# A hybrid attention and delta-net block on one core: w_out by token rows with resident, pre-gated slabs

## The chip, the core and the metric

The kernel runs on one core of a Trainium2 chip. A core has a matrix engine (TensorE, "PE" in the profile, with its weight loads shown as "PEld"), three engines for elementwise work (VectorE "DVE", ScalarE "ACT", GpSimd "POOL"), and SyncE ("SP"), which here issues most of the transfers between HBM and the on-chip memory SBUF. Matrix products land in PSUM, eight banks of 128 partitions by 512 floats. Every engine runs its own list of instructions in order and waits on semaphores for the others.

The metric is the device time of one execution in microseconds (us), the median of the runs shown; lower is better. A profile is one further execution, recorded by the hardware.

## What is computed

One transformer block for 1024 tokens of width D = 1024, in float32. A vector c modulates it: `mod` is silu(c) times a matrix `w_ada` plus `b_ada`, cut into six vectors of width 1024. Left out below are the two mixers, a dilated attention (8 heads of 64) and a gated delta rule (8 heads of 64).

```python
def _rmsnorm(x, g):
    x32 = x.astype(jnp.float32)
    y = x32 * lax.rsqrt(jnp.mean(x32 * x32, axis=-1, keepdims=True) + EPS)
    return (y * g.astype(jnp.float32)).astype(x.dtype)
...
        mod = c_act @ w_ada[l] + b_ada[l]
        sh1, sc1, g1, sh2, sc2, g2 = [m[:, None, :] for m in jnp.split(mod, 6, axis=-1)]
        h = _rmsnorm(x, norm_attn_g[l]) * (1.0 + sc1) + sh1
...
        y = jnp.concatenate([y_attn, y_delta], axis=-1) @ w_out[l]
        x = x + g1 * y
        h = _rmsnorm(x, norm_ffn_g[l]) * (1.0 + sc2) + sh2
        y = (jax.nn.silu(h @ w_gate[l]) * (h @ w_up[l])) @ w_down[l]
        x = x + g2 * y
    return _rmsnorm(x, final_norm_g)
```

The change concerns the product with `w_out`, the gate `g1` behind it and the norm, scale and shift that make h for the feed-forward part.

## The kernel before

**Products.** Each float32 operand is split into a high part that TensorE takes in one pass (fp32r) and the low remainder, and a product is the sum of three: high by high, high by low, low by high. One instruction multiplies a stationary 128x128 tile with a moving 128x512 tile. `wsplit` (L228) brings a slab of weights of 128 x 512: SP's transfer, ACT's cast to the high part, POOL's subtraction for the low part (L237).

**Stages.** Projections and the delta rule run first (to about 470 us). Then comes attention: 32 units, four pairs of heads by eight query blocks. A unit's scores are made by `att_score`, normalised on POOL (tile X, L1273), transposed one unit later by `att_turn` (L1285, blocks "tr"), and multiplied with the values three units later by `att_value` (L1301). Between those products TensorE is given others: a generator in `fill[0]`, from which `ahead` draws as many steps as a share of time allows. Up to unit 8 (`i == free`) these are leftover projections; at that point a change of hands takes place: old pools close, the operands yh and yl (the mixers' outputs, transposed, high and low) are allocated and loaded, and the filler becomes `out_delta`.

**w_out in two phases.** `out_delta` multiplies the delta half of y with its half of w_out, 16 groups of 12 products, each giving one tile [128 output columns, 512 tokens]: the weights are stationary and y moves. DVE multiplies the group with the gate (a column of `mod`) and adds x (L1367); the result goes to HBM (`xp`). After attention, phase 2 (L1481 to L1541) does the same for the attention half, 16 groups in order of token half and column block d, each slab of weights loaded again for each half; DVE multiplies with the gate and adds the loaded `xp` tile (L1492). Each x tile is also turned to rows by four transposes two groups later (`x2_turn`, L1449) and written to HBM as `x2`.

**The norm by columns.** Since a tile holds columns on its partitions, the sum of squares over D runs across partitions: ACT squares, POOL and DVE accumulate (L1504), eight matmul records take the sum for four token blocks (L1514), then a root and a reciprocal, a diagonal tile dg (L1517) and a product with ones that spreads the factors over the partitions (rsb, L1521). `normed2` applies factor and scale on DVE (L1533) and the shift on ACT (L1536), in place.

**After w_out.** H11 and H21 are the split halves of the first 512 tokens' h; the gate and up products of the first two column blocks ("early", L1700, through `gate_first`, `up_first` and `up_mm`, L1574) need only these. The rest of the up and gate products uses sums of blocks in the manner of Strassen: DVE makes T1, T2, T3, T4 and H22 from the x2 tiles by subtractions and splits (L1705 on; lines L1580, L1583 and L1470). The second half's `normed2` calls stand in the loop that makes T2. Then the feed-forward network runs to the end.

**Modulation.** `mod_in` loads one 128x512 tile of w_ada ("wm"), `mod_add` adds its product with c to an accumulator on DVE (L1335), and every eighth addition `mod_out` sums over partitions by four products with ones (L1345). 16 additions stand before the attention loop, then one per iteration from the third on.

**Order.** A scheduler orders instructions by the program's order and by priorities: code under `urgent()` goes ahead, and `tc.issue_after` puts transposes behind a named product. So each engine's list, which is fixed before the kernel runs, decides who waits behind whom.

Of the kernel before, what the change touches and what calls it, by code (L numbers as in the profile page):

```python
# [88 lines left out]
def build(tc, I, out):  # L89
# [68 lines left out]
    def tbank(name):  # L158
        return psb(name, "t", 2)
# [32 lines left out]
    G2 = const([P, KT], "G2")  # L192
    R_d = dr.tile([8, 1152], F32, name="R_d")
# [340 lines left out]
    class _:  # L534
# [13 lines left out]
        xp = scratch("xp", 2 * KT, [P, HALF])  # L548
# [78 lines left out]
    def z_evac(g):  # L627
        def f(tb, ps):
            zt = pv.tile([P, 256], F32, name=f"zt{g}_{tb}", tag="zt", bufs=4)
# [457 lines left out]
    def va_evac(c):  # L1087
        def f(tb, ps):
            t = pv.tile([P, 256], F32, name=f"va{c}_{tb}", tag="vt", bufs=4)
# [5 lines left out]
    def spill(name, dst):  # L1095
        def f(hf, ps):
            for i in range(2):
                t = pv.tile([P, 256], F32, name=f"sp_{name}_{hf}_{i}", tag="vt", bufs=4)
# [99 lines left out]
    for tag, n, w in (  # L1198
        ("X", XB, T), ("raw", 2, T), ("QS", 3, T), ("KS", 3, T), ("va", 2, T), ("KL", 3, T), ("et", ETB, T),
        ("ng", 2, T), ("xo", 3, HALF), ("wm", 4, HALF),  # L1200
# [119 lines left out]
    def mod_in(n):  # L1320
        if n < 64:
            i, k = n // KT, n % KT
            t0 = 16 + 4 * i
            p, b = (pa, 4) if i < 6 else (po2, 2)
            mod_w[n] = p.tile([P, HALF], F32, name=f"wm_{i}_{k}", tag="wm", bufs=b)
# [13 lines left out]
    def mod_out(i):  # L1339
        t0 = 16 + 4 * i  # L1340
        acc = states[:, HALF * (i % 2) : HALF * (i % 2) + HALF]
        ps = tbank(f"mods{i}")
        v = acc.rearrange("p (t j m) -> p j t m", j=4, m=32)
# [4 lines left out]
        t = (pv if i < 6 else po2).tile([P, 256], F32, name=f"mt{i}", tag="zt", bufs=4 if i < 6 else 1)  # L1348
# [6 lines left out]

    def out_delta():

        for d in range(KT):
            slabs = [(wsplit(I["wo"][d, 1], 512, f"wo{d}_1"), 4)]
            for hf in range(2):  # L1360
                cs = slice(hf * HALF, (hf + 1) * HALF)
                xo = pa.tile([P, HALF], F32, name=f"xo{d}_{hf}", tag="xo", bufs=3)
                nc.sync.dma_start(xo, I["xT"][d * P : (d + 1) * P, cs])
                ps = gbank(f"wo{d}_1_{hf}")
                yield from gemm(ps, slabs, yh, yl, cs)
                with urgent():
                    nc.vector.scalar_tensor_tensor(  # L1367
                        out=xo, in0=ps, scalar=mod[:, 16 + d : 17 + d], in1=xo, op0=ALU.mult, op1=ALU.add,
                    )
                nc.sync.dma_start(_.xp[2 * d + hf], xo)  # L1370
# [14 lines left out]
    for n in range(4):  # L1385
        mod_in(n)
    ahead(LEAD)
    for n in range(16):
        mod_add(n)
        mod_in(n + 4)  # L1390
    for i in range(len(units) + AV):
        if i >= AV:
            mod_add(16 + i - AV)
        if i == free:
            run(fill[0])
            share[0] = 0.0
            sh_.close()
            py, sy = pool("py", side="right")
# [24 lines left out]
        if i in (1, 2):  # L1423
            mod_out(i - 1)
        if i >= AV:
            if 20 + i - AV < 48:
                mod_in(20 + i - AV)
            if (i - AV) % 8 == 7:
                mod_out(2 + (i - AV) // 8)
# [6 lines left out]
    run(fill[0])  # L1436

# [7 lines left out]
    def x2_turn(d, hf, t):  # L1445

        ps = tbank(f"x2t{d}_{hf}")
        for b in range(4):
            nc.tensor.transpose(ps[:, b * P : (b + 1) * P], t[:, b * P : (b + 1) * P], ident)  # L1449
        xt = px.tile([P, 4, P], F32, name=f"xt2_{d}_{hf}", tag="m", bufs=5)  # L1450
        nc.scalar.copy(xt.rearrange("p b d -> p (b d)"), ps)
        nc.sync.dma_start(
            _.x2[hf][:, :, d * P : (d + 1) * P].rearrange("b p d -> p b d"), xt
        )

    behind = []
    x2 = {}
# [18 lines left out]
    acc = px.tile([P, HALF], F32, name="acc2_0", tag="m", bufs=5)  # L1476
# [4 lines left out]
    for hf in range(2):  # L1481
        cs = slice(hf * HALF, (hf + 1) * HALF)
        if hf == 1:
            acc = px.tile([P, HALF], F32, name="acc2_1", tag="m", bufs=5)
        for d in range(KT):
            slabs = [(wsplit(I["wo"][d, 0], 512, f"wo{d}_0_{hf}"), 0)]
            t = x2[d, hf]
            nc.sync.dma_start(t, _.xp[2 * d + hf])
            ps = (gbank, sbank)[d % 2](f"wo{d}_0_{hf}")
            run(gemm(ps, slabs, yh, yl, cs))  # L1490
            with urgent():
                nc.vector.scalar_tensor_tensor(  # L1492
                    out=t, in0=ps, scalar=mod[:, 16 + d : 17 + d], in1=t, op0=ALU.mult, op1=ALU.add,
                )
            behind.append((d, hf, t))
            if len(behind) > 2:
                with tc.issue_after(last[0].ins):
                    x2_turn(*behind.pop(0))
            if d == 0:
                nc.scalar.activation(acc, t, AF.Square)  # L1500
            else:
                sq = px.tile([P, HALF], F32, name=f"sq2_{hf}_{d}", tag="m", bufs=5)
                nc.scalar.activation(sq, t, AF.Square)
                (nc.vector if d > 5 else nc.gpsimd).tensor_tensor(out=acc, in0=acc, in1=sq, op=ALU.add)  # L1504
        while behind:
            x2_turn(*behind.pop(0))

        ps, pb = ybank(f"ssq2_{hf}"), abank(f"rsb2_{hf}")
        r4 = r8[:, 4 * hf : 4 * hf + 4]
        rs = po.tile([P, HALF], F32, name=f"rs2_{hf}", tag="p1", bufs=4)  # L1510
        dg = po.tile([P, 4, P], F32, name=f"dg2_{hf}", tag="p1", bufs=4)
        with urgent():
            for tb in range(4):
                nc.tensor.matmul(ps[:, tb : tb + 1], acc[:, tb * P : (tb + 1) * P], ones[:, 0:1], start=True, stop=True)  # L1514
            nc.scalar.activation(r4, ps[:, 0:4], AF.Sqrt, bias=eps1, scale=1.0 / D)
            nc.vector.reciprocal(r4, r4)
            nc.vector.tensor_tensor(  # L1517
                out=dg, in0=ident.unsqueeze(1).to_broadcast([P, 4, P]),
                in1=r4.unsqueeze(2).to_broadcast([P, 4, P]), op=ALU.mult,
            )  # L1520
            nc.tensor.matmul(pb, ones, dg.rearrange("p b t -> p (b t)"), start=True, stop=True)  # L1521
            nc.scalar.copy(rs, pb)
        if hf == 1:
            sy.close()
            spv.close()
            wq, swq = pool("wq", side="right")
            pt, st_ = pool("pt", side="right")
            for name in ("H22", "T1", "T2", "T3", "T4"):
                h2_block(pt, name)

        def normed2(d):
            t = x2[d, hf]
            nc.vector.scalar_tensor_tensor(  # L1533
                out=t, in0=t, scalar=G2[:, d : d + 1], in1=rs, op0=ALU.mult, op1=ALU.mult
            )
# [426 lines left out]
```

## Time and profile before

| | us |
|---|---|
| median of 3 runs (1408.3 to 1410.0) | 1409.6 |
| the profiled execution | 1412.03 |
| its span, first to last instruction | 1410.3 |
| TensorE busy | 1344.1 (95%) |
| VectorE busy | 930.7 (66%) |
| ScalarE busy | 660.5 (47%) |
| GpSimd busy | 291.2 (21%) |
| mean granted TensorE clock | 0.987 of full speed |

How to read the rows that follow: a group row gives line, engine, operation, `output<-inputs`, shapes and count, then busy us and mean ns of one, then the idle time of the engine just before them and what ended it. A timeline row gives start, duration, engine, line and tiles, in brackets the idle time before it and its releaser. A row of waits reads "who waited for whom: us in total, times, longest". The chain of waits follows back from the last instruction to what released each step.

### The profile page before, as it was taken

To read this page: it belongs to the slowest core of one execution; us is meant where nothing else is said; L and a number is where in the kernel's file an instruction comes from. 1 tells how busy PE (TensorE), PEld (TensorE's weight loads), DVE (VectorE), ACT (ScalarE), POOL (GpSimd) and SP (SyncE) were. 2 spreads that over 40 slices of the span, in tenths; PEclk is the share of its full clock that TensorE was granted. 3 is DMA by queue.
4 is the path that set the end of the run, shared out by engine and by line. 5 is a ranking of instruction groups with operands and counts; after the bars stand their busy time and mean duration, and the time that the engine had idled before them with its cause. 6 is when DMAs were issued, how large, how long until landed. Compare 5 with 4: busy or idle time off the path is not lost.

```text
span 1410.3 us, 23618 instructions
## 1 busy us (share of the span) xinstructions
PE 1344.1 (95%) x8536; PEld 1106.0 (78%) x8536; DVE 930.7 (66%) x1739; ACT 660.5 (47%) x1274; POOL 291.2 (21%) x262
## 2 busy tenths in 40 slices
PE   7998999999998899999999799999999999999997
PEld 4776887888898777777877588888888888888886
DVE  3687694658546266866549986767575776474487
ACT  3487434374333446555568433333333333444446
POOL 2335432434314433444351000000000000000000
PEclk9999899999999999999999899999999999999999
DMA  8645334463403887673274375545363665766677
GB/s 305 219 132 163 90 115 132 129 186 87 131 24 100 261 254 243 211 223 120 79 225 131 124 220 172 166 142 185 114 217 110 201 208 180 264 214 201 195 221 244
DMA packets 171342, 244.59 MB, mean 173 GB/s; under 512 B 33014, under 2 KB 76327, under 8 KB 171224
## 3 DMA queue, kind: packets, MB, share of 16 engines
q1 hardware_dynamic: 156504, 231.53, 52.2%
q10 hardware_dynamic: 14720, 11.54, 2.5%
q8 instruction: 67, 1.10, 0.3%
q14 instruction: 51, 0.42, 0.1%
HBM read 180.25 MB, written 67.48 MB: 176 GB/s over the span
## 4 chain that ended last, share of the span: by engine, by line
PE 67%; DVE 15%; DMA 8%; issue 4%; ACT 3%; POOL 2%; SPq 1%; ACTq 0%; DVEq 0%; POOLq 0%
PE wua L1574 8%; PE wga L1574 8%; PE X L1777 7%; PE wuc L1574 4%; PE Z L1777 4%; PE wgc L1574 4%; PE wo L595 4%; PE g_a L595 2%; DMA wm<-in_wada 2%; PE Y L1777 2%; DVE tm L894 2%; DVE tt L898 2%; PE wgb L1574 2%; PE wub L1574 2%; PE f L257 2%
## 5 line engine op out<-in xcount | busy, mean ns | idle before, releaser
L1564 DVE TENSOR_TENSOR wl_db<-wr_db,wh_db 128x512 fp32r<-128x512 f32 x77 | 53.2, 691 | 75.6 <-ACT wh_db L1563 75.4
L1563 ACT CAST wh_db<-wr_db 128x512 fp32r<-128x512 f32 x77 | 47.9, 622 | 98.0 <-PE X L1777 42.9
L1271 ACT ACTIVATE X<-X,sc 128x128 f32<-128x128 f32 (+7 forms) x64 | 49.7, 777 | 71.5 <-DVE sc L1266 60.8
L1273 POOL TENSOR_SCALAR X<-X,sc 128x128 f32<-128x128 f32 (+7 forms) x64 | 51.6, 807 | 112.4 <-DVE sc L1272 83.2
L1777 PE MATMUL X<-wl_db,wh_da 128*128 128x512 f32 x176 | 68.7, 390 | 0.3 <-DVE wl_db L1564 0.2
L1777 PE MATMUL X<-wh_db,wl_da 128*128 128x512 f32 x176 | 68.5, 389 | 0.0
L1777 PE MATMUL X<-wh_db,wh_da 128*128 128x512 f32 x176 | 68.4, 389 | 0.0
L1335 DVE SCALAR_TENSOR_TENSOR states<-wm,cc,states 128x512 f32<-128x512 f32 x56 | 46.5, 831 | 17.0 <-DMA wm<-in_wada 16.2
L595 PE MATMUL wo<-yh,wh_wo 128*128 128x512 f32 x128 | 54.0, 422 | 0.0
L1564 DVE TENSOR_TENSOR wl_da<-wr_da,wh_da 128x512 fp32r<-128x512 f32 x77 | 52.8, 686 | 1.7 <-ACT wh_da L1563 1.7
L1266 DVE CUSTOM_DVE_ANT_0 X<-S,ng 128x512 f32<-128x512 f32 (+3 forms) x64 | 37.4, 585 | 22.2 <-PE S L1263 18.4
L595 PE MATMUL g_a<-hh,wh_a 128*128 128x512 f32 x128 | 51.4, 401 | 0.0
L595 PE MATMUL wo<-yh,wl_wo 128*128 128x512 f32 x128 | 51.2, 400 | 0.0
L595 PE MATMUL wo<-yl,wh_wo 128*128 128x512 f32 x128 | 51.0, 398 | 0.0
L595 PE MATMUL g_a<-hh,wl_a 128*128 128x512 f32 x128 | 50.8, 397 | 0.0
L595 PE MATMUL g_a<-hl,wh_a 128*128 128x512 f32 x128 | 50.7, 396 | 0.0
L1563 ACT CAST wh_da<-wr_da 128x512 fp32r<-128x512 f32 x77 | 47.4, 616 | 6.5 <-PE wua L1574 5.8
L1285 PE MATMUL tr<-ident,X 128*128 128x128 f32 x288 | 43.7, 279 | 6.1 <-DVE et L1288 4.8
L1563 ACT CAST wh_wg_s<-wg_s 128x512 fp32r<-128x512 f32 x33 | 20.5, 623 | 59.9 <-PE wuc L1574 22.6
L1285 PEld LDWEIGHTS tr<-ident,X 128*128 128x128 f32 x288 | 33.0, 141 | 14.8 <-issue 3.6
L1563 ACT CAST wh_wg<-wr_wg 128x512 fp32r<-128x512 f32 x33 | 20.5, 622 | 51.1 <-PE wua L1574 18.9
L1563 ACT CAST wh_wu_s<-wu_s 128x512 fp32r<-128x512 f32 x33 | 20.4, 621 | 49.6 <-PE wga L1574 16.7
(527 smaller groups left out, 4377.0 us busy)
## 6 DMA issues: line engine op xcount, KB each, us to landing
wr_da<-ao_d SPq DMA_DIRECT2D x77, 256.0 KB, 3.2
wm<-in_wada SPq DMA_DIRECT2D x64, 256.0 KB, 3.8
wr_wg<-in_wg SPq DMA_DIRECT2D x48, 256.0 KB, 2.9
wr_wu<-in_wu SPq DMA_DIRECT2D x48, 256.0 KB, 2.7
ao_d<-a SPq DMA_DIRECT2D x44, 256.0 KB, 2.7
wr_wd<-in_wdn SPq DMA_DIRECT2D x44, 256.0 KB, 3.2
wr_db<-wt_d SPq DMA_DIRECT2D x44, 256.0 KB, 3.2
ao_d<-as SPq DMA_DIRECT2D x33, 256.0 KB, 2.0
```

Of the source, the lines that this page charges most:

```text
L257: nc.tensor.matmul(first[bank], a[:, w0], b[k][:, cs], start=(k == 0 and n_ == 0), stop=(k == KT - 1 and n_ == 2))
L595: last[0] = nc.tensor.matmul(ps, a[:, w0], b[k0 + k4][:, cs], start=(i == 0), stop=(i == n - 1))
L894: nc.vector.tensor_tensor(out=tv, in0=bc(nt[:, j, j + 1 : 32], j + 1), in1=tt[:, j, 0 : j + 1].unsqueeze(1).to_broadcast([P, m, j + 1]), o ...
L1266: nc.vector.tensor_tensor_reduce(out=X[:, c0:c1], in0=ps[:, 0 : c1 - c0], in1=ng[:, u + c0 : u + c1], scale=1.0, scalar=(3e38 if m is None ...
L1271: nc.scalar.activation(X[:, 0:nk], X[:, 0:nk], AF.Exp, scale=-1.0, bias=m, accum_out=sc[:, 2:3])
L1273: nc.gpsimd.tensor_scalar(out=X[:, 0:nk], in0=X[:, 0:nk], scalar1=sc[:, 3:4], scalar2=0.0, op0=ALU.mult, op1=ALU.add)
L1285: nc.tensor.transpose(ps[:, (kb - c0) * P : (kb - c0 + 1) * P], X[:, kb * P : kb * P + P], ident)
L1335: nc.vector.scalar_tensor_tensor(out=acc, in0=w, scalar=cc[:, k : k + 1], in1=acc, op0=ALU.mult, op1=ALU.add)
L1563: nc.scalar.copy(hi, src)
L1564: (eng or nc.vector).tensor_tensor(out=lo, in0=src, in1=hi.bitcast(F32), op=ALU.subtract)
L1574: nc.tensor.matmul(ps, a[:, w0], b, start=(first and k == 0 and n_ == 0), stop=(k == 3 and n_ == 2), skip_group_check=True,)
L1777: nc.tensor.matmul(bank[b], a[:, ts_], w, start=(first and f == 0 and n_ == 0), stop=(f == NF - 1 and n_ == 2), skip_group_check=True,)
```

## The change

- w_out's products give [128 tokens, 512 columns]: y's block is now stationary and the slab of weights moves. For each half of the columns (s = 0, 1) four slabs of 128x512 are held for all eight token blocks, so that there are 16 slabs in all.
- The gate is multiplied into the slabs: POOL multiplies the raw slab with `g1r`, the gate spread over all partitions, before ACT's cast and POOL's subtraction. `g1r` comes from the first two `mod_out`, now one product each of a 128x128 tile of ones with the 128x512 accumulator, added to a broadcast of b_ada.
- x is loaded, and `xp` and `x2` are written, by rows of tokens.
- Norms by rows: ACT's square sums over its row as it goes, then a few operations on 128x1, and ACT scales the row (`out_row`). `out_turn` transposes the scaled row into two banks of four blocks and takes each block out with scale and shift, ACT and DVE in turn.
- The token blocks 0 to 3 are done for s = 0, then for s = 1, then blocks 4 to 7 each for both. A block's transposes follow a product group later; the last block's follow the first early gate products. `normed2` leaves the loop that makes T2.
- All 16 slabs are allocated where attention runs (three pools); to make room, the buffers zt and vt fall from 4 to 3 and wm from 4 to 2, with `mod_in` two steps ahead in place of four. 8 additions stand before the loop and the others are spread over it.

```diff
@@ mod_out
+        if i < 2:
+            cs = slice(HALF * i, HALF * i + HALF)
+            nc.tensor.matmul(ps, ones, acc, start=True, stop=True)
+            nc.vector.tensor_tensor(out=g1r[:, cs], in0=ps, in1=g1r[:, cs], op=ALU.add)
+            return
...
+    def out_slab(k, s):
+
+        n = slabs_made[0]
+        slabs_made[0] += 1
+        p, h, b = (pe, "e", 4) if n >= 12 else (wp, "w", 5) if n % 7 < 5 else (pr, "v", 2)
+        raw = wp.tile([P, slot], F32, name=f"wr_wo{k}_{s}", tag="wr", bufs=3)
+        hi = p.tile([P, slot], F32R, name=f"wh_wo{k}_{s}", tag=f"{h}h", bufs=b)
+        lo = p.tile([P, slot], F32R, name=f"wl_wo{k}_{s}", tag=f"{h}l", bufs=b)
+        with urgent():
+            nc.sync.dma_start(raw, I["wo"][k * P : (k + 1) * P, columns(s)])
+            nc.gpsimd.tensor_tensor(out=raw, in0=raw, in1=g1r[:, columns(s)], op=ALU.mult)
+            nc.scalar.copy(hi, raw)
+            nc.gpsimd.tensor_tensor(out=lo, in0=raw, in1=hi.bitcast(F32), op=ALU.subtract)
+        return hi, lo
+
+    def out_mm(ps, slabs, k0, tb):
+
+        ts_ = slice(tb * P, (tb + 1) * P)
+        for k, (wh, wl) in enumerate(slabs):
+            for n, (a, b) in enumerate(((yh, wh), (yh, wl), (yl, wh))):
+                last[0] = nc.tensor.matmul(
+                    ps, a[k0 + k][:, ts_], b, start=(k == 0 and n == 0), stop=(k == 3 and n == 2)
+                )
+            yield 0.64
+
     def out_delta():
 
-        for d in range(KT):
-            slabs = [(wsplit(I["wo"][d, 1], 512, f"wo{d}_1"), 4)]
-            for hf in range(2):
...
+        for s in range(2):
+            slabs = [out_slab(4 + k, s) for k in range(4)]
+            for tb in range(TB):
+                xo = pa.tile([P, HALF], F32, name=f"xo{tb}_{s}", tag="xo", bufs=3)
+                nc.sync.dma_start(xo, I["x"][tb * P : (tb + 1) * P, columns(s)])
+                ps = gbank(f"wo{tb}_1_{s}")
+                yield from out_mm(ps, slabs, 4, tb)
                 with urgent():
...
+                    nc.vector.tensor_tensor(out=xo, in0=ps, in1=xo, op=ALU.add)
+                nc.sync.dma_start(_.xp[tb][:, columns(s)], xo)
...
-    for n in range(4):
+    nc.sync.dma_start(g1r, I["bada1"].to_broadcast([P, D]))
+    summed = [0]
+
+    def mod_until(n):
+        while summed[0] < n:
+            mod_add(summed[0])
+            if summed[0] < 46:
+                mod_in(summed[0] + 2)
+            summed[0] += 1
+            if summed[0] % 8 == 0:
+                turns_out.append(summed[0] // 8 - 1)
+
+    turns_out = []
+    for n in range(2):
         mod_in(n)
     ahead(LEAD)
-    for n in range(16):
-        mod_add(n)
-        mod_in(n + 4)
+    mod_until(8)
     for i in range(len(units) + AV):
-        if i >= AV:
-            mod_add(16 + i - AV)
+        while turns_out:
+            mod_out(turns_out.pop(0))
+        mod_until(9 + i if i < free else 16 + -(-32 * (i - free + 1) // (len(units) + AV - free)))
...
+    def out_row(tb):
+
+        t, r = xt[tb], rq[:, tb]
+        hs = pq.tile([P, D], F32, name=f"hs{tb}", tag="hs", bufs=2)
+        with urgent():
+            nc.vector.tensor_tensor(out=r[:, 2:3], in0=r[:, 0:1], in1=r[:, 1:2], op=ALU.add)
+            nc.scalar.activation(r[:, 2:3], r[:, 2:3], AF.Sqrt, bias=eps1, scale=1.0 / D)
+            nc.vector.reciprocal(r[:, 3:4], r[:, 2:3])
+            for s in range(2):
+                nc.scalar.mul(hs[:, columns(s)], t[:, columns(s)], r[:, 3:4])
+        nc.sync.dma_start(_.x2[tb // 4][tb % 4], t)
+        return hs
+
+    def out_turn(tb, hs):
...
+        for q in range(2):
+            ps = tbank(f"x2t{tb}_{q}")
+            for j in range(4):
+                d = 4 * q + j
+                nc.tensor.transpose(ps[:, j * P : (j + 1) * P], hs[:, d * P : (d + 1) * P], ident)
+            with urgent():
+                for j in range(4):
+                    d = 4 * q + j
+                    if j % 2:
+                        nc.vector.tensor_scalar(
+                            out=x2[d, hf][:, ts_], in0=ps[:, j * P : (j + 1) * P],
+                            scalar1=G2[:, d : d + 1], scalar2=mod[:, 24 + d : 25 + d], op0=ALU.mult, op1=ALU.add,
+                        )
+                    else:
+                        nc.scalar.activation(
...
+    slabs = [[out_slab(k, s) for k in range(4)] for s in range(2)]
+    rows = []
+    order = [(tb, s) for s in range(2) for tb in range(4)] + [(tb, s) for tb in range(4, TB) for s in range(2)]
+    for n, (tb, s) in enumerate(order):
+        if s == 0:
+            xt[tb] = pq.tile([P, D], F32, name=f"xt{tb}", tag="xt", bufs=5)
+            nc.sync.dma_start(xt[tb], _.xp[tb])
+        ps = (gbank, sbank)[n % 2](f"wo{tb}_0_{s}")
+        run(out_mm(ps, slabs[s], 0, tb))
         with urgent():
...
+            nc.vector.tensor_tensor(out=xt[tb][:, columns(s)], in0=ps, in1=xt[tb][:, columns(s)], op=ALU.add)
+            sq = pq.tile([P, HALF], F32, name=f"sq{tb}_{s}", tag="sq", bufs=1)
+            nc.scalar.activation(sq, xt[tb][:, columns(s)], AF.Square, accum_out=rq[:, tb, s : s + 1])
+        if rows and rows[0][2] < n:
+            b, hs, _n = rows.pop(0)
+            with tc.issue_after(last[0].ins):
+                out_turn(b, hs)
...
+        if s == 1:
+            rows.append((tb, out_row(tb), n + 1 - (tb < 4)))
...
-    early = [{w: gate_first(f, w) for w in ("wg", "wu")} for f in range(AHEADF)]
+    early = [{} for f in range(AHEADF)]
+    for f in range(AHEADF):
+        for w in ("wg", "wu"):
+            early[f][w] = gate_first(f, w)
+            if rows:
+                b, hs, _n = rows.pop(0)
+                with tc.issue_after(last[0].ins):
+                    out_turn(b, hs)
...
     for k in range(4):
-        normed2(k)
-        normed2(4 + k)
         sub(x2[k, 0], x2[k, 1], x2[k, 0])
```

More of the change, by code (lines that the diff above doesn't have):

```diff
@@ L1353, in mod_out, with columns @@
             )
-    def out_delta():
-        for d in range(KT):
-            slabs = [(wsplit(I["wo"][d, 1], 512, f"wo{d}_1"), 4)]
-            for hf in range(2):
[L1361 to L1365, printed above, removed]
+    def columns(s):
+        return slice(s * HALF, (s + 1) * HALF)
@@ L1444, in build @@
     px, sx = pool("px")
[L1445 to L1457, printed above, removed]
+    pq, sq_ = pool("pq")
+    x2, xt = {}, {}
+    rq = po.tile([P, TB, 4], F32, name="rq", tag="rq", bufs=1)
+    def out_row(tb):
[10 more added lines that the diff above has]
+    def out_turn(tb, hs):
+        hf, ts_ = tb // 4, slice(tb % 4 * P, tb % 4 * P + P)
+        for q in range(2):
[13 more added lines that the diff above has]
+                        nc.scalar.activation(
+                            x2[d, hf][:, ts_], ps[:, j * P : (j + 1) * P], AF.Identity,
+                            bias=mod[:, 24 + d : 25 + d], scale=G2[:, d : d + 1],
+                        )
     HB = {}
@@ L1479, in build @@
             x2[d, hf] = px.tile([P, HALF], F32, name=f"x2_{d}_{hf}", tag=f"x{i}", bufs=4)
[L1481 to L1511, printed above, removed]
-        with urgent():
[L1513 to L1535, printed above, removed]
-            nc.scalar.activation(t, t, AF.Identity, bias=mod[:, 24 + d : 25 + d])
-        if hf == 0:
-            for d in range(KT):
-                normed2(d)
-                h2_split(("H11", "H21")[d // 4], d % 4, x2[d, 0], nc.vector)
```

54 lines of the change are left out of this document (31 added, 23 removed).

## The prediction

> **What bounds the kernel now.** I read the table by stretches first (core 0; length, then busy us of PE, PEld, DVE, ACT, POOL, then the granted TensorE clock, DMA share and GB/s).
>
> ```profile
> 556.00:698.50 142.50, 137.78 (x1082) 108.63 (x1080) 96.65 (x271) 81.55 (x173) 57.51 (x60) 1.00 0.52 158
> 698.50:754.30 55.80, 53.41 (x267) 43.14 (x263) 32.09 (x40) 36.37 (x63) 28.95 (x21) 1.00 0.66 207
> 754.30:780.00 25.70, 24.22 (x112) 19.42 (x110) 22.56 (x38) 20.70 (x37) 0.00 (x0) 1.00 0.45 123
> 780.00:803.00 23.00, 14.18 (x50) 10.52 (x48) 22.97 (x40) 8.40 (x15) 0.00 (x0) 0.85 0.26 92
> 803.00:830.00 27.00, 26.78 (x111) 22.08 (x112) 25.89 (x44) 9.90 (x18) 0.00 (x0) 0.94 0.76 227
> 830.00:1130.00 300.00, 300.00 (x1336) 247.59 (x1335) 205.32 (x325) 109.83 (x190) 0.00 (x0) 1.00 0.52 166
> ```
>
> The rows are, in order, attention with the delta half of w_out in its gaps; the attention half of w_out; the first gate and up products; the operands of the split product, made on DVE; and the rest. TensorE is the bound everywhere but in 780 to 803, where DVE is busy 22.97 of 23.00 us and PE 14.18. The chain of waits says the same (start, length, piece):
>
> ```profile
> 766.48 0.67 DVE x L1533
> ...
> 802.56 0.61 DVE wg_u L1583
> 803.22 4.60 PE wga L1574 x12
> 807.82 2.72 PE wua L1574 x12
> ```
>
> From 766.48 its pieces are DVE's alone, up to 802.56; then PE goes on. So what shortens PE work before 754, or DVE's list from there to 803, shortens the kernel, and what makes PE wait in 556 to 698 lengthens it: PE idles there for only 142.50 - 137.78 = 4.7 us. From 803 on the work is the same in both kernels and I carry it over.
>
> **Part 1: phase 2 of w_out as [token, column].** The product count stays 192. In the timeline of PE a group of 12 and the four transposes behind it come every 3.22 us:
>
> ```profile
> 698.56 0.50 PE L595 MATMUL wo<-yh,wh_wo 128*128 128x512 f32 x1
> ...
> 706.86 0.60 PE L1449 MATMUL x2t<-ident,x 128*128 128x128 f32 x4
> ...
> 710.08 0.60 PE L1449 MATMUL x2t<-ident,x 128*128 128x128 f32 x4
> ...
> 754.29 0.47 PE L1574 MATMUL wga<-H11h,wh_wg 128*128 128x512 f32 x1
> ```
>
> The first 36 products take 706.86 - 698.56 = 8.30 us, hence 0.231 each at most and 2.72 per 12 (the chain row at 807.82); the four transposes are 3.22 - 2.72 = 0.50. Sixteen groups are 43.5, sixteen sets of four transposes 8.0, together 51.5 of the 55.7 us between 698.56 and 754.29. The rest is the sum of squares, its broadcast, and stalls. The first two are PE instructions of the norm by columns; the stalls stand in the list of PE's waits for 698 to 810 (who, for whom; us, times, longest):
>
> ```profile
> L1514 PE MATMUL ssq<-onesr,acc 128*128 128x1 f32 x16 | 2.0, 244 | 0.0
> L1521 PE MATMUL rsb<-dg,onesr 128*128 128x512 f32 x4 | 2.2, 640 | 0.6 <-DVE dg L1517 0.6
> PE wga L1574 <- ACT wg_u L1627: 4.3, 1, 4.3
> PE wga L1574 <- DVE wg_u L1583: 3.7, 1, 3.7
> PE x2t L1449 <- ACT xt L1451: 1.7, 1, 1.7
> ```
>
> After the change the norm is taken by rows, with no PE instruction. The transposes still are 16 sets of four, but the last token block's two sets now stand among the gate products, as two sets (1.0 us) and the second half's norm did before; so phase 2 holds 43.5 + 14 x 0.50 = 50.5 us if nothing makes it wait. Gain: 55.7 - 50.5 = 5.2 us.
>
> Does anything make it wait? Two sets are evacuated as eight 128x128 blocks, ACT and DVE in turn, each waiting for the other because they share a bank. The trace of before has no such block with scale and shift out of PSUM. From below:
>
> ```profile
> L1271 ACT ACTIVATE X<-X,sc 128x128 f32<-128x128 f32 x8 | 3.2, 401 | 4.9 <-DVE sc L1266 4.9
> L1288 DVE COPY et<-tr 128x128 f32<-128x128 f32 x8 | 2.3, 286 | 0.1
> L1536 ACT ACTIVATE x<-x,mod 128x512 f32<-128x512 f32 x16 | 11.2, 720 | 2.4 <-DVE x L1533 2.3
> L1492 DVE SCALAR_TENSOR_TENSOR x<-wo,mod,x 128x512 f32<-128x512 f32 x16 | 11.9, 746 | 19.2 <-PE wo L595 14.5 <-DMA x<-xp_d 4.7
> ```
>
> 4 x 0.401 + 4 x 0.286 = 2.7 us; from above, as if each block cost as much as a four times wider one, 4 x 0.720 + 4 x 0.746 = 5.9 us. A token block of the second half gives PE 2 x 2.72 + 1.0 = 6.4 us. Even the dear end fits, so I take no stall and keep 2 us for the range (that is the 1.7 of the old x2t stall, rounded up). ACT's share of a row (two squares, two scalings at 0.72 at most, a root, four blocks) is about 5 us, under 6.4 as well. The first product group waits for slabs made during attention, priced in part 3.
>
> **Part 2: the operand chain.** Eight normed2 steps of the second half leave DVE's list between the first gates and 803, where DVE has no gap:
>
> ```profile
> L1533 DVE SCALAR_TENSOR_TENSOR x<-x,G,rs 128x512 f32<-128x512 f32 x16 | 14.4, 930 | 1.8 <-ACT rs L1522 1.8
> 762.00 2.07 DVE L1533 SCALAR_TENSOR_TENSOR x<-x,G,rs 128x512 f32<-128x512 f32 x3
> ...
> 803.08 1.28 DVE L1564 TENSOR_TENSOR wl_wu_s<-wu_s,wh_wu_s 128x512 fp32r<-128x512 f32 x2
> ```
>
> At 2.07 us for three they are 8 x 0.66 = 5.3 us (less their overlap). Before, the chain starts 762.00 - 754.29 = 7.7 us after the first gate product and ends 48.8 us after it. After, the last token block's transposes stand behind the first 24 gate products (5.4 us); eight blocks and the handovers follow, and by my walk along DVE's and ACT's order the first subtraction of the chain comes some 11.8 us after the first gate. It has 48 operations to the last T4 and then six, at about 0.6 us each: 11.8 + 32.2 = 44.0. Gain: 48.8 - 44.0 = 4.8 us. Bounds: 0 (the blocks and the silu's table load come so late that they eat the eight steps) and 5.3. PE idles in this stretch both times, so the slow restart (4.60 against 2.72 us at 803.22) stays in.
>
> **Part 3: what attention pays.** The gate's first two mod_out become one 128x512 broadcast each. Before, four 128x32 products are
>
> ```profile
> 696.31 0.42 PE L1345 MATMUL mods<-states,onesr 128*32 128x128 f32 x8
> ...
> 759.97 1.11 PE L1521 MATMUL rsb<-dg,onesr 128*128 128x512 f32 x2
> ```
>
> and the row at 759.97 is the same product as the new one: 2 x (1.1 - 0.42) = +1.4 us on PE.
>
> The slabs fall from 24 to 16, but all 16 are now made before attention ends, and each has a multiply on POOL besides its subtraction: 32 POOL operations where about 13 stood, at
>
> ```profile
> L237 POOL TENSOR_TENSOR wl_wo<-wr_wo,wh_wo 128x512 fp32r<-128x512 f32 x19 | 25.5, 1340 | 24.2 <-ACT wh_wo L236 12.7 <-DMA x<-xp_d 9.0 <-PE x2t L1449 2.6
> ```
>
> so 19 x 1.3 = +25 us on an engine that is busy 57.5 of 142.5 us: it fits as a sum, but not everywhere. POOL also normalises the scores X, in order, and PE transposes them, in order. POOL before, where the filler changes hands:
>
> ```profile
> 551.15 2.21 POOL L1273 TENSOR_SCALAR X<-X,sc 128x1024 f32<-128x1024 f32 x2 [1.79 <-DVE sc L1272]
> 555.79 0.37 POOL L1273 TENSOR_SCALAR X<-X,sc 128x128 f32<-128x128 f32 x1 [2.42 <-DVE sc L1272]
> 556.75 0.38 POOL L1273 TENSOR_SCALAR X<-X,sc 128x128 f32<-128x128 f32 x1 [0.59 <-DVE sc L1272]
> ...
> 560.40 0.27 PE L1285 MATMUL tr<-ident,X 128*128 128x128 f32 x1
> ```
>
> In the new order three multiplies stand behind the X that ends at 553.36, then the X of 555.79, then three subtractions and three multiplies whose raw slabs can be fetched only when those subtractions have freed the three buffers, and only then the X of 556.75. Three multiplies end at 557.3, the first X at 557.7, the subtractions at 561.6; the raw slabs come about 3 us after their buffers, so the multiplies end near 566.1 and the second X at 566.5. PE's transpose, at 560.40 before, waits behind it, and everything of PE behind that. At most 566.5 - 560.4 = 6.1 us, nothing if PE has as much other work ahead of it. PE now has the first 12 products of the delta half and two more ahead; I take 4 us. Two later bunches of nine and eight POOL operations fall on stretches with units 4.7 us apart, which I give 1 us together (0 to 6).
>
> wm's lookahead falls from 4 tiles to 2. DVE waits in order for these:
>
> ```profile
> L1335 DVE SCALAR_TENSOR_TENSOR states<-wm,cc,states 128x512 f32<-128x512 f32 x56 | 46.5, 831 | 17.0 <-DMA wm<-in_wada 16.2
> wm<-in_wada SPq DMA_DIRECT2D x64, 256.0 KB, 3.8
> ```
>
> Two tiles cover about 9 us at the new pace, against 3.8 to landing, and only 8 additions instead of 16 crowd ahead of the loop: 0, within -3 to +3. DVE's evacuations lose the scale and stay at 0.75. SP issues 2 MB less of slabs, one 512 KB row of x instead of two halves, and x2 in whole rows; DMA is busy 0.66 of phase 2, so that is cover, not gain: 0. The buffers zt and vt (4 to 3) are emptied by transfers before their turn comes again: 0.
>
> **A rule against the change.** Beside POOL, DVE's step with two SBUF inputs takes 930 ns in the mean and 0.66 to 0.74 without it (rows of L1533). The Trainium skill (SBUF — State Buffer, "Who interferes with whom") says that a DVE instruction with two SBUF inputs and a GpSimd instruction that reads SBUF exclude one another for a whole instruction. The rows agree; by the rule, the new 25 us of POOL in attention would hold up its 32 wm additions by up to about 0.6 us each, 19 us of DVE at the most, on an engine idle for 46 us there. It speaks for the first rival below, whose bunches would be longer still.
>
> **Sum.** -5.2 - 4.8 + 1.4 + 4 + 1 = -3.6 us. The profiled execution took 1412.0 us (span 1410.3), so 1408.4; the median of the runs is 2.4 below it, so 1406.0.
>
> **Rivals.** (a) POOL's queue decides. Its bunches are exposed at 6 us each: two of them give 12 + 1.4 - 10.0 = +3.4, about 1413, and three +9.4, about 1419; each restart as at 803.22 adds 4.60 - 2.72 = 1.9. It turns from gain to loss once attention ends more than 10 us late. For it: PE's 4.7 idle us in 142, so nothing absorbs a late X. Against: POOL's idle time is twice the new work. (b) The chain's gain doesn't come: the last block's turn is late by the table load and DVE waits as long as it saved. Then -5.2 + 6.4 = +1.2, about 1410. For it: one block turned behind the first gates gates the whole chain. (c) The hand-over is hidden by PE's products: -10.0 + 1.4 = -8.6, about 1401. For it: 14 products lie ahead.
>
> TensorE idle behind a late X may cost more than the wait: the restart at 803.22 shows it, at a clock of 0.85 in that stretch. The Trainium skill (TensorE: Matmul & The Clock Gate, "What's actually happening") puts the array at half clock after an idle window of about 3.4 us; the waits of 3.7 and 4.3 us agree. By it my 4 us at the hand-over would be 5.9, and the sum 1407.9.
>
> **Numbers.** Forecast 0.42, (a) 0.25, (b) 0.15, (c) 0.18. A difference of 0.2%, 2.8 us, is about what a measurement of this kernel can tell. Faster than 1406.8: all of (c) and somewhat over two thirds of the forecast, 0.50; slower than 1412.4: (a) and a little of the rest, 0.29; between them 0.21. The range, 1398 to 1417, takes in (c) with the 2 us of part 2, and (a) with two bunches and their restarts; the forecast's own range is 1402 to 1410.
>
> **What would show it.** Phase 2 from its first product to the first gate in 50 to 52 us; the first gate to PE's resumption in 44 to 45; the end of attention 5 to 8 us later than 698.56, with a PE wait of some 4 us for a POOL X near 560. It would be wrong if PE waits for blocks or rows inside phase 2, if DVE idles ahead of the chain beyond 12 us, or if PE waits for X or slabs all through the later attention.

## The result, and the profile after

The changed kernel is slower: 1416.0 us, median of 10 runs (1410.9 to 1426.4), against 1409.0 us for the kernel before on the same chip (1406.1 to 1412.3, 10 runs). The ratio is 1.0055, with a 95% interval of 1.0031 to 1.0080. Its profiled execution has a span of 1417.3 us against 1410.3, also 7.0 us more, so the two traces can be compared term by term.

The table by stretches of the changed kernel, cut at its own marks: 716.2 is the first product of phase 2, 765.5 the first gate product, 809.8 the point where PE goes on after DVE's operand chain. The columns are those of the prediction.

```profile
450.00:716.20 266.20, 238.43 (x1574) 186.62 (x1573) 151.68 (x384) 128.37 (x275) 123.66 (x111) 0.96 0.63 187
...
716.20:765.50 49.30, 49.30 (x250) 40.49 (x244) 28.46 (x69) 36.74 (x90) 0.00 (x0) 1.00 0.47 166
765.50:803.00 37.50, 33.95 (x143) 27.30 (x142) 34.43 (x64) 24.05 (x46) 0.00 (x0) 0.92 0.30 85
```

The first stretch of the kernel before, from the same start to its own first product of phase 2:

```profile
450.00:698.50 248.50, 234.03 (x1592) 185.10 (x1591) 150.11 (x390) 128.93 (x274) 101.53 (x96) 0.99 0.65 197
```

And two pieces of the changed kernel's chain of waits (start, length, piece):

```profile
809.17 0.61 DVE wg_u L1620
...
809.83 4.61 PE wga L1611 x12
```

Phase 2 is shorter, 765.5 - 716.2 = 49.3 us against 55.7, and PE is busy in all of it. From the first gate product to PE's resumption it is 809.8 - 765.5 = 44.3 us against 48.9. From there to the end it is 607.5 against 607.1. The gains are there, 11.0 us together. The loss is all ahead of them: attention ends 17.7 us later. Of that, 4.4 us are PE's busy time (238.43 - 234.03; 2.4 of them are the gate sums, below, and the granted clock in the stretch is 0.96 against 0.99) and 13.3 us are idle time (27.8 against 14.5 us).

Where does the lag arise? In both kernels POOL normalises 64 score tiles in the same order, so the times at which it ends them can be set side by side (us, from the timelines of POOL):

| score tile | before | after | lag |
|---|---|---|---|
| 1st | 482.2 | 478.7 | -3.5 |
| 7th | 514.9 | 520.7 | +5.8 |
| 16th, the last ahead of the change of hands | 553.4 | 560.7 | +7.3 |
| 18th, the second behind it | 557.1 | 578.3 | +21.2 |
| 22nd | 573.8 | 584.9 | +11.1 |
| 64th | 693.1 | 709.4 | +16.3 |

So two places carry most of it: about 9 us between the first and the seventh tile, and some 4 us that stay of a 14 us jolt at the change of hands; another 5 us come bit by bit behind it.

**The first place.** PE's waits of the changed kernel in 470 to 720, and PE's timeline at the longest:

```profile
PE mods L1346 <- DVE states L1336: 7.3, 1, 7.3
PE S L1264 <- DVE sc L1268: 5.6, 5, 3.0
PE wo L1387 <- DVE yl L1411: 3.7, 3, 1.8
PE tr L1287 <- ACT et L1292: 3.1, 6, 0.8
PE tr L1287 <- POOL X L1275: 2.7, 3, 1.1
...
500.11 2.08 PE L1346 MATMUL mods<-states,onesr 128*128 128x512 f32 x2 [7.26 <-DVE states L1336]
```

PE stands for 7.3 us ahead of the first gate sum, because DVE's additions for it wait for wm tiles. The eight additions start between 479.5 and 499.3, 2.8 us apart, where the kernel before makes eight in 10.2 us (482.5 to 492.7). The seventh starts 7.4 us after SP issued the load of its tile, with the DMA engines busy for 0.96 of the time from 493 to 500; SP's row, then DVE's:

```profile
490.50 1.80 SPq L1327 DMA_DIRECT2D wm<-in_wada  x2
```

```profile
497.88 0.75 DVE L1336 SCALAR_TENSOR_TENSOR states<-wm,cc,states 128x512 f32<-128x512 f32 x1 [4.09 <-DMA wm<-in_wada]
```

DVE's waits for wm in the whole stretch, after, then before:

```profile
DVE states L1336 <- DMA wm<-in_wada: 30.6, 18, 5.6
```

```profile
DVE states L1335 <- DMA wm<-in_wada: 12.8, 12, 2.6
```

In the kernel before PE also waits ahead of its first gate sum, but less, and for the softmax on DVE:

```profile
494.62 0.43 PE L1345 MATMUL mods<-states,onesr 128*32 128x128 f32 x8 [3.20 <-DVE sc L1272]
```

So some 4 us of the wait are new. The sum itself costs 2.08 us where the four small products cost 0.43. SP, which loads the tiles, then stands still for 7 us at a slab, because the buffer that it loads into is freed by a subtraction of POOL (tile wl_a) that stands in POOL's list behind two multiplies and another subtraction, and the multiplies wait for that same sum (DVE adds it to g1r from 502.22 to 502.91). DVE's longest wait for wm, 5.6 us, ends at 514.8, behind this standstill. SP's timeline, then POOL's:

```profile
503.33 0.33 SPq L1327 DMA_DIRECT2D wm<-in_wada  x1
510.33 0.33 SPq L1376 DMA_DIRECT2D wr_wo<-in_wo  x1
510.76 0.37 SPq L1327 DMA_DIRECT2D wm<-in_wada  x1
```

```profile
503.05 2.65 POOL L1377 TENSOR_TENSOR wr_wo<-wr_wo,g1r 128x512 f32<-128x512 f32 x2 [3.67 <-issue]
...
508.56 1.74 POOL L239 TENSOR_TENSOR wl_a<-wr_a,wh_a 128x512 fp32r<-128x512 f32 x1
```

**The second place.** POOL's timeline at the change of hands, after:

```profile
561.91 4.29 POOL L1377 TENSOR_TENSOR wr_wo<-wr_wo,g1r 128x512 f32<-128x512 f32 x3 [1.22 <-DVE g1r L1347]
566.18 0.81 POOL L1275 TENSOR_SCALAR X<-X,sc 128x128 f32<-128x128 f32 x1
566.96 4.64 POOL L1379 TENSOR_TENSOR wl_wo<-wr_wo,wh_wo 128x512 fp32r<-128x512 f32 x3
571.55 3.41 POOL L1377 TENSOR_TENSOR wr_wo<-wr_wo,g1r 128x512 f32<-128x512 f32 x2
575.20 1.45 POOL L1377 TENSOR_TENSOR wr_wo<-wr_wo,g1r 128x512 f32<-128x512 f32 x1 [0.23 <-DMA wr_wo<-in_wo]
577.97 0.37 POOL L1275 TENSOR_SCALAR X<-X,sc 128x128 f32<-128x128 f32 x1 [1.32 <-DVE sc L1274]
```

This is the bunch of the prediction, in its order, but the second score tile waits 1.32 us more, for DVE. What DVE does in the meantime is five splits of y, 1.7 us each, and POOL's two multiplies at 571.55 take 1.7 us each as well, where two took 2.65 together at 503.05:

```profile
568.71 8.48 DVE L1411 TENSOR_TENSOR yl<-yl,yh 128x512 fp32r<-128x512 f32 x5
```

The ten splits of y as groups, after and before:

```profile
L1411 DVE TENSOR_TENSOR yl<-yl,yh 128x512 fp32r<-128x512 f32 x10 | 13.1, 1336 | 0.5 <-ACT yh L1410 0.5
```

```profile
L1378 DVE TENSOR_TENSOR yl<-yl,yh 128x512 fp32r<-128x512 f32 x10 | 6.7, 702 | 0.8 <-ACT yh L1377 0.8
```

Six of the eight splits at the change of hands take 1.75 us. So DVE is late beside POOL's bunch, PE waits for DVE (3.7 us of PE's waits are for these very splits), and the reciprocal that the next score tile needs stands behind them in DVE's list.

### The profile page after: what moved, and what is told of

Read it like the earlier page. It is cut to its first block, busy times and chain, and to the rows that moved or that the text cites. A ratio compares the mean times of both kernels' runs of the same rounds, so it can differ in the third digit from the quotient of the medians.

```text
span 1417.3 us, 23510 instructions
## 1 busy us (share of the span) xinstructions
PE 1341.3 (95%) x8504; PEld 1103.1 (78%) x8504; DVE 926.0 (65%) x1761; ACT 658.3 (46%) x1302; POOL 286.9 (20%) x260
## 4 chain that ended last, share of the span: by engine, by line
PE 67%; DVE 13%; DMA 8%; ACT 4%; issue 4%; POOL 3%; SPq 0%; ACTq 0%; DVEq 0%; POOLq 0%
PE wua L1611 8%; PE wga L1611 8%; PE X L1820 7%; PE wo L1387 5%; PE wuc L1611 4%; PE Z L1820 4%; PE wgc L1611 4%; DMA wm<-in_wada 3%; PE g_a L597 3%; PE g_va L620 3%; PE Y L1820 2%; PE wub L1611 2%; PE wgb L1611 2%; PE g_vd L597 2%; PE vd L505 1%
## 5 line engine op out<-in xcount | busy, mean ns | idle before, releaser
L1387 PE MATMUL wo<-wh_wo,yl 128*128 128x512 f32 x128 | 51.0, 398 | 3.7 <-DVE yl L1411 3.7
L1387 PE MATMUL wo<-wh_wo,yh 128*128 128x512 f32 x128 | 54.0, 422 | 0.5 <-ACT yh L1410 0.5
L1268 DVE CUSTOM_DVE_ANT_0 X<-S,ng 128x512 f32<-128x512 f32 (+3 forms) x64 | 37.4, 585 | 21.2 <-PE S L1265 16.0
L1387 PE MATMUL wo<-wl_wo,yh 128*128 128x512 f32 x128 | 51.2, 400 | 0.0
```

The lines of the kernel that those rows point to most:

```text
L1268: nc.vector.tensor_tensor_reduce(out=X[:, c0:c1], in0=ps[:, 0 : c1 - c0], in1=ng[:, u + c0 : u + c1], scale=1.0, scalar=(3e38 if m is None ...
L1387: last[0] = nc.tensor.matmul(ps, a[k0 + k][:, ts_], b, start=(k == 0 and n == 0), stop=(k == 3 and n == 2))
```

## The experiments

Three theories stood at the start. *Supply*: two wm tiles with two steps of lookahead feed DVE too slowly. *Gate*: slabs that wait for the finished gate hold SP's queue. *Load* or *contention*: the multiplies on POOL come in bunches ahead of the score tiles and hinder DVE. Ratios are to the kernel before on the same chip, which ran at 1407.6 to 1408.7 in these comparisons.

**wm4.** Four wm tiles again.

```diff
-        ("ng", 2, T), ("xo", 3, HALF), ("wm", 2, HALF),
+        ("ng", 2, T), ("xo", 2, HALF), ("wm", 4, HALF),
...
-            if summed[0] < 46:
-                mod_in(summed[0] + 2)
+            if summed[0] < 44:
+                mod_in(summed[0] + 4)
```

> The changed kernel with four wm tiles and four steps of lookahead again; to make room the xo tiles go from 3 to 2 and the small mt tile takes an xo buffer. Supply theory (DVE waits for wm tiles and everything in order behind it is late): the wait of DVE for wm falls from 35 towards 16 us, PE's 7.3 us wait for the first gate sum shrinks to 3 or less, and the time falls by 6 to 10 us to 1406 to 1410. Gate theory (slabs wait for the finished gate and hold SP's queue) and load theory (POOL has too much to do): 1414 to 1416, the PE wait stays.

1411.9 us, ratio 1.0032 (1.0006 to 1.0057). DVE's wait for wm falls to 11.2 us and PE's wait for the first sum to 3.0. The time lies between the ranges of the theories. It is a third to a half of the loss, but the interval overlaps that of the changed kernel (1.0031 to 1.0080), so the time alone doesn't show it; the waits do. The hand-over stays, with a PE wait of 3.05 us for a score tile there. Supply is a cost, but not the only one.

**g_early.** The slabs are multiplied by the bias part of the gate only.

```diff
-            nc.vector.tensor_tensor(out=g1r[:, cs], in0=ps, in1=g1r[:, cs], op=ALU.add)
+            nc.vector.tensor_tensor(out=acc, in0=ps, in1=g1r[:, cs], op=ALU.add)
```

> The changed kernel with the slabs multiplied by the bias part of the gate alone (the sum of the modulation product is computed but not added into the gate), so that no slab waits for it; the same number of POOL operations. Gate theory: SP's queue is freed earlier, wm tiles come earlier, 1408 to 1411. Load theory: 1415 to 1416, no change. Supply theory: DVE's waits for wm stay, 1413 to 1416.

1412.3 us (1405.2 to 1417.0), ratio 1.0000 (0.9974 to 1.0026). The runs lie so far apart that the median and the ratio tell different stories. PE's wait for the sum is 4.5 us, DVE's for wm 23.0, in a profile that fell on the slowest of the ten runs. It leans to the gate theory but doesn't settle its size.

**nogate.** The multiplies are left out, and with them the gate.

```diff
-            nc.gpsimd.tensor_tensor(out=raw, in0=raw, in1=g1r[:, columns(s)], op=ALU.mult)
```

> The changed kernel without the 16 multiplies of the slabs by the gate (the gate is left out of the result). Load theory: 22 us of POOL work gone, the late score tile at the hand-over comes in time, 1404 to 1408. Gate theory: the same or a little less, 1404 to 1410. Supply theory: the stretch 480 to 525 stays 7 us late, only the hand-over's part comes back, 1411 to 1414.

1404.9 us, ratio 0.9988 (0.9963 to 1.0012). Without the multiplies the loss is gone, although DVE still waits 24.4 us for wm and PE 4.3 us for the first sum. In its profile attention ends at 699.7, where the kernel before has 698.6.

**b_wm2.** The kernel before with two wm tiles.

```diff
-        ("ng", 2, T), ("xo", 3, HALF), ("wm", 4, HALF),
+        ("ng", 2, T), ("xo", 3, HALF), ("wm", 2, HALF),
...
-        mod_in(n + 4)
+        mod_in(n + 2)
```

> The kernel before with two wm tiles and two steps of lookahead, nothing else. Supply theory: DVE's waits for wm rise from 16 to 30 us or more and attention ends 6 to 10 us later: 1415 to 1419. Gate and load theory: unchanged within 2 us, 1407 to 1411.

1417.4 us (five runs), ratio 1.0067 (1.0042 to 1.0092). DVE's wait for wm rises from 12.8 to 25.0 us. In this kernel, with 16 additions ahead of its loop, the shorter lookahead costs 9 us by itself. The edit that the prediction costed at nothing is dear where it is made alone. In the changed kernel, with its other spread of the additions, four tiles win back only 3 to 4 us; that the spread is the reason is not shown.

**b_burst.** Nine idle POOL products in the kernel before, at the change of hands.

```diff
+            with urgent():
+                for _n in range(9):
+                    nc.gpsimd.tensor_tensor(
+                        out=dum, in0=yl[4][:, 0:HALF].bitcast(F32), in1=yh[4][:, 0:HALF].bitcast(F32), op=ALU.mult
+                    )
             fill[0] = out_delta()
```

> The kernel before with nine added POOL products of 128x512 (two SBUF inputs, result unused) where the filler changes hands, ahead of and between the score tiles of the next two units, where the changed kernel has its six multiplies and three subtractions. Contention theory (POOL's bunch and DVE's splits of y exclude one another, and the score tile behind them comes late): the splits of y go from 0.7 to 1.1 us or more in the mean, the second score tile is 5 to 12 us late and attention ends 3 to 6 us later, 1412 to 1415. Supply theory (only wm matters): 1407 to 1410.

1417.5 us, ratio 1.0063 (1.0044 to 1.0082). The bunch alone costs 9 us (four runs), more than either theory gave it. The products, and the splits of y beside them:

```profile
L1409 POOL TENSOR_TENSOR dum<-yl,yh 128x512 f32<-128x512 f32 x9 | 12.9, 1432 | 2.1 <-DVE yl L1379 1.6
```

```profile
L1379 DVE TENSOR_TENSOR yl<-yl,yh 128x512 fp32r<-128x512 f32 x10 | 10.7, 1097 | 0.9 <-ACT yh L1378 0.9
```

The splits go from 0.70 to 1.10 us in the mean, and PE waits 4.1 us for score tiles where before it waited 0.2.

**b_fill.** The same POOL time, but written only.

```diff
+                nc.gpsimd.tensor_tensor(out=dum, in0=..., in1=..., op=ALU.mult)
+                for _n in range(28):
+                    nc.gpsimd.memset(dum, 0.0)
```

> The kernel before with one added POOL product and 28 memsets of 128x512 where the run with nine added products had its bunch: about the same POOL time (1.3 + 28 x 0.48 = 14.7 us against 13.4), at the same urgency, but nothing read from SBUF. Exclusion theory (DVE and POOL shut each other out when both read SBUF twice): DVE's splits of y stay near 0.7 us and the time is 1408 to 1411. Queue theory (the score tiles come late behind any POOL work): as with the nine products, 1413 to 1418.

1412.5 us, ratio 1.0031 (1.0008 to 1.0053): half of the nine products' cost, between the two theories, and the intervals overlap. Its splits of y keep their length beside 14.7 us of memsets:

```profile
L1379 DVE TENSOR_TENSOR yl<-yl,yh 128x512 fp32r<-128x512 f32 x10 | 6.7, 696 | 1.2 <-ACT yh L1378 1.2
...
L1410 POOL MEMSET dum<- 128x512 f32 x28 | 14.7, 525 | 1.1
```

So DVE's splits stretch beside POOL's products and not beside its memsets; that is shown. How the price of a bunch divides is not, because the two bunches are not alike in POOL's list: the memsets stretch over 25 us (555.5 to 580.7), the products over 15.5 (551.0 to 566.5), and the 18th score tile falls 1.1 us further behind the 16th than in the kernel before, with the products 5.9 us.

**nogate_wm4.** Four wm tiles and no multiplies (edits of wm4 and nogate).

> The changed kernel with four wm tiles (and two xo tiles) and without the 16 multiplies by the gate (the gate is left out of the result). If supply and contention are two separate costs they add: 1416 - 4 (four wm tiles) - 11 (no multiplies) = 1401, and attention ends at 692 to 697 in the profile. If they are one cost seen twice: 1404 to 1406, as without the multiplies alone.

1407.8 us, ratio 0.9992 (0.9967 to 1.0017), no better than without the multiplies alone, 0.9988, and above both forecasts. Where no slab waits for the gate, the number of wm tiles doesn't show in the time. A loss through the two xo tiles isn't excluded.

**gdve_wm4.** Four wm tiles, and the multiplies on DVE.

```diff
-            nc.gpsimd.tensor_tensor(out=raw, in0=raw, in1=g1r[:, columns(s)], op=ALU.mult)
+            nc.vector.tensor_tensor(out=raw, in0=raw, in1=g1r[:, columns(s)], op=ALU.mult)
```

> The changed kernel with four wm tiles and the multiplies on DVE instead of POOL (0.69 us each instead of 1.3). Contention theory: POOL's bunches go, but DVE takes 11 us of work in order and waits there for slabs; 1402 to 1407. Supply theory: as with four wm tiles alone, 1410 to 1413.

1404.6 us, ratio 0.9975 (0.9962 to 0.9989): faster than both kernels, with the full result. Its PE waits in 470 to 700, and its stretches:

```profile
PE mods L1346 <- DVE states L1336: 3.2, 1, 3.2
PE S L1264 <- DVE sc L1268: 2.5, 4, 1.0
PE tr L1287 <- DVE et L1290: 1.9, 4, 1.0
PE tr L1287 <- POOL X L1275: 1.8, 3, 0.9
```

```profile
450.00:699.10 249.10, 233.45 (x1569) 183.06 (x1568) 157.55 (x400) 129.57 (x275) 105.63 (x95) 0.99 0.64 198
699.10:748.10 49.00, 49.00 (x247) 40.30 (x243) 28.47 (x69) 36.67 (x90) 0.00 (x0) 1.00 0.46 167
```

Attention now ends at 699.1, phase 2 keeps its 49.0 us.

**gdve.** The multiplies on DVE alone (the edit of gdve_wm4's diff, two wm tiles).

> The changed kernel with the 16 multiplies by the gate on DVE instead of POOL and nothing else (two wm tiles stay). Contention theory: nearly the whole gain of the two edits together, 1404 to 1407. If the supply of wm tiles is a cost of its own: 1408 to 1412.

1408.5 us, ratio 1.0005 (0.9984 to 1.0027). Half a per cent of the time, 7 us, comes back by this edit alone; with four wm tiles as well 0.8%, 11 us; with four wm tiles alone 0.2%, 3 us. With the multiplies kept, the two gains add up within the intervals (0.0050 and 0.0023 of the time alone, 0.0080 together).

**gdve_wm3.** Multiplies on DVE, three wm tiles, three xo tiles.

> The multiplies on DVE and three wm tiles with three steps of lookahead, the xo tiles at three as in the changed kernel. If four wm tiles cost something through the two xo tiles: 1401 to 1404; if not, 1404 to 1406 as with four.

1405.9 us, ratio 0.9977 (0.9955 to 0.9999): as with four wm tiles and two xo tiles. A cost of two xo tiles doesn't show, though a gain by the third xo tile and a loss by the missing fourth wm tile could hide one another.

**gdve_wm4_late.** As gdve_wm4, with the gate sums taken from the third unit on.

```diff
-        while turns_out:
+        while turns_out and i > 1:
             mod_out(turns_out.pop(0))
```

> The multiplies on DVE, four wm tiles, and the first gate sum placed two units later on PE, where before had it one later. If PE's 3 us wait for that sum is a loss: 1401 to 1404. If the slabs behind the gate then come late, or PE's wait only moves: 1404 to 1407.

1404.1 us, ratio 0.9959 (0.9936 to 0.9982), the best of all; its interval and that of gdve_wm4 overlap, so the last step is not shown to help. PE's wait for the sum stays (2.7 us) and now ends with DVE's softmax instead of a wm tile, as in the kernel before.

**Where each edit helps.** The score tiles place each run's lag. Each cell is what a run falls behind the kernel before from one tile to the other (us, one profiled execution each). Ahead of the 16th tile nothing is changed in b_burst and b_fill, which show -0.9 and +1.0 there, so differences of about 2 us mean nothing.

| run | gate multiplies | wm tiles | 1st to 16th tile | 16th to 22nd | 22nd to 64th |
|---|---|---|---|---|---|
| changed kernel | POOL | 2 | +10.8 | +3.8 | +5.1 |
| g_early | POOL | 2 | +7.8 | +3.6 | +2.4 |
| gdve | DVE | 2 | +5.1 | +1.6 | +3.9 |
| nogate | none | 2 | +4.2 | -0.1 | +2.0 |
| gdve_wm3 | DVE | 3 | +3.3 | +2.1 | -0.7 |
| wm4 | POOL | 4 | -0.3 | +5.7 | +6.1 |
| gdve_wm4 | DVE | 4 | +0.8 | +2.6 | +1.5 |
| gdve_wm4_late | DVE | 4 | -1.1 | +2.6 | +0.7 |
| nogate_wm4 | none | 4 | +1.0 | +0.4 | +4.1 |
| b_wm2 | as before | 2 | +5.0 | -3.1 | +7.1 |
| b_burst | as before, nine products added | 4 | -0.9 | +3.2 | +5.8 |
| b_fill | as before, memsets added | 4 | +1.0 | +2.1 | +0.6 |

Ahead of the change of hands, four wm tiles remove the lag wherever the multiplies are, and with two it is about halved when POOL has no multiplies. From the 16th tile to the 64th the changed kernel's variants fall back 6.0 to 11.8 us with the multiplies on POOL and 1.4 to 5.6 without. The buffers zt and vt stay at three in all of them, so they cost nothing that shows ahead of the change of hands. The nine added products bring 5.8 us behind the 22nd tile, where that kernel has no further bunch, so the lag that comes bit by bit can be an after-effect of the first bunch. How it comes about is open.

## Why the prediction was wrong

It forecast 1406, 3 us faster, and the kernel is 7 us slower. The 1416.0 lies near the upper end of its range only because rival (a) was taken into it. The gains were right; the step that failed is the third part of the sum, "what attention pays": 1.4 + 4 + 1 + 0 = 6.4 us forecast, 17.7 measured. Most of the difference stands in the two terms put at 0 and 1 us.

- **Phase 2: -5.2 forecast, -6.4 measured.** No stall came, as forecast. Two sets of transposes run back to back, so that eight take 765.46 - 764.66 = 0.80 us instead of 2 x 0.50. Blocks out of PSUM with scale and shift cost 0.41 us on DVE and 0.45 on ACT, nearer to the low than to the high ends taken for them:

```profile
764.66 1.04 PE L1511 MATMUL x2t<-ident,hs 128*128 128x128 f32 x8
765.46 0.48 PE L1611 MATMUL wga<-H11h,wh_wg 128*128 128x512 f32 x1
...
L1516 DVE TENSOR_SCALAR x<-x2t,G,mod 128x128 f32<-128x128 f32 x32 | 12.4, 408 | 4.0 <-ACT x L1521 4.0
...
L1521 ACT ACTIVATE x<-x2t,mod,G 128x128 f32<-128x128 f32 x32 | 13.6, 454 | 1.7 <-PE x2t L1511 1.2 <-DVE x L1516 0.3
```

- **The operand chain: -4.8 forecast, -4.6 measured.** The way there was not quite as walked: the first subtraction came 7.3 us after the first gate product (772.74), not 11.8, with the last token block's blocks and the silu's table load behind and around it; the last block was out at 777.0, 11.5 us after, and from there DVE's list ran on with 0.5 us of idle time. Rival (b) fell.
- **Gate sums: +1.4 forecast, +2.4 measured.** The two take 3.2 us (the group row below; the four small products they replace took 0.42 to 0.43 each time). The row taken for the forecast, 1.11 us, ran among other products; the second sum is like it (1.13 us at a granted clock of 1.00), the first takes 2.08 us behind 7.3 idle us, and in wm4 behind 3.0, at a clock of 0.50 both times. That is a slow restart as the prediction feared it for the hand-over, in a place where it expected no wait:

```profile
L1346 PE MATMUL mods<-states,onesr 128*128 128x512 f32 x4 | 3.2, 893 | 7.3 <-DVE states L1336 7.3
```

- **wm's lookahead: "0".** The changed kernel falls back 10.8 us from the 1st to the 16th score tile; 2.4 of them are the gate sums' own length. The average distance of two tiles, 9 us, was set against a median of 3.8 us to landing. But for the first sum the additions follow one another more closely, so that two tiles cover 2 x 2.8 = 5.6 us, and a tile could be used up to 7.4 us after its issue. Behind the first sum, SP issues these loads in order behind slabs whose buffers wait for POOL's multiply, and the multiply waits for the gate sum that the wm tiles feed. With four tiles the 10.8 us are gone in the trace, and the time falls by 3 to 4 us; in the kernel before, two tiles instead of four cost 9 us. The prediction named what queues behind DVE's wait, but not what queues ahead of the load on SP.
- **"I take 4 us" at the hand-over, "1 us together" for the later bunches.** The first size was about right, 3.8 us that stay at the 22nd tile, but in part by luck. From the end of the 16th tile to the second behind it the walk through POOL's list gave 566.5 - 553.4 = 13.1 us, and it took 578.3 - 560.7 = 17.6, because the walk counted POOL's own time alone. It left out that DVE has eight splits of y to make at just that moment and that six of them take 1.75 us instead of 0.7 beside POOL's products, which become longer too. The prediction laid its "rule against the change" on the wm additions, which it took to have slack; it belonged on the splits, which PE waits for. Behind the 22nd tile another 5.1 us came where 1 was taken. Moving the multiplies to DVE won 7 us in all, in its trace 5.7 us ahead of the 16th tile and 3.4 behind it; nine idle products at the hand-over cost 9 us in the kernel before.

Rival (a) had the sign and, at 1413 to 1417 with two exposed bunches, the size; its place was half right. The first 9 us arise before any of its bunches, around the wait for the first gate sum. Its argument, that PE's 4.7 idle us absorb nothing, held. How the first place splits between the wm tiles and SP's standstill stays open: more wm tiles remove its lag, and multiplies off POOL's list halve it, so the two depend on one another.

## What to carry to other kernels

A sum of busy time on a half-idle engine says nothing about a bunch: look at what the engine has to deliver in order behind the bunch, and at what its neighbour does in the same microseconds. When buffers of a prefetch are halved, follow the queue that issues it, and every wait ahead of the load in that queue, not the mean time to landing. Work that is moved to win time in one stage may be worth moving again, to the engine that is faster at it: the multiplies on DVE (0.72 us each in the trace of gdve, against 1.3 to 1.7 on POOL in the changed kernel) and the tiles given back turn a loss of 0.55% into a gain of 0.25%.

## What the runs showed of the hardware

The splits of y on DVE, which read two operands from SBUF, took 0.70 us in the mean of ten beside 28 POOL memsets, 1.10 with nine POOL products of two operands among them, and 1.34 in the changed kernel, where five of them in a row took 1.7 each and POOL's multiplies beside them 1.7 instead of 1.3. The Trainium skill (SBUF — State Buffer, "Who interferes with whom") states this difference, that a GpSimd instruction that only writes does not contend. These runs agree: beside the memsets the splits took 0.70 us, as in the kernel before. What a bunch's reads cost in the kernel's time is not shown apart from its lateness.
